# RWKV and HGRN steps placed between the W_in GEMMs by a clock instead of a table: a hybrid decoder layer on one core

## The chip, the cores and the metric

One core of one Trainium2 chip runs the whole step. The metric is the device time of one execution in microseconds (us). The kernel before was run three times; the profile shown is of one further execution with the profiler on.

## The reference

One decoder layer for 512 prompt tokens and 8 sequences of 4 sample tokens, all in f32 (D_MODEL 1024):

```
h = RMSNorm(x)
u = h @ W_in                      # 46 blocks of 128 columns: q,f,i,g | r,k,v, low-rank | gates
o_a = HGRN2(u_a)                  # 4 heads, state 128x128, chunkwise gated recurrence
o_b = RWKV7(u_b, h_prev)          # 8 heads, state 64x64, delta-rule update, group norm, gate
x = x + (sig(g_a)*(o_a @ W_a_out) + sig(g_b)*(o_b @ W_b_out)) @ W_out
x = x + relu(RMSNorm(x) @ W_up)^2 @ W_down
y = RMSNorm(x)
```

The outputs are y and the new states of both branches.

## The kernel before

**GEMMs.** Tokens lie along the free axis: 544 columns (512 prompt, 32 sample), split in two halves of 272. Each weight block of 128 columns is loaded by SP into a tile of the tag "stage" (NST buffers); `split` (L166) rounds it to `whi` on ACT and writes the rest `wlo = st - whi` on DVE, one pass over 128x1024 each. `gemm_h` (L398) makes three products per block (`h_hi,whi`, `h_hi,wlo`, `h_lo,whi`), so one W_in block (`in_unit`, L410) is 2 halves x 3 products x 8 = 48 matmuls of 128x272 in the type fp32r. There are 46 such units. After them come `half_unit` for W_b_out and W_a_out, then W_out, W_up and W_down (tiles `full_unit_ps` and `pd`).

**Background.** Between these GEMMs the two recurrences run as small f32 matmuls (32 to 128 wide) with much DVE, ACT and some POOL work. They are Python generators that yield after each step. RWKV goes in two groups of two head pairs (`rw_all`, L990): `rw_batch` (inputs and head sums), `rw_inverse` (triangular inverses on DVE), `rw_solve`, `rw_affine`, `rw_chain` (L793, eight chunk steps that each depend on the last, then the outputs `rw_chain_py`), `gn` (group norm on DVE) and `rw_out`, which stores the branch output to the DRAM tile `ob_d`. HGRN goes by head (`hg_head`, L1080): a scan, seven levels of `decayed` on DVE, score matmuls `hg_head_pl`, and an output stored to `oa_d`. `rw_sample` and `hg_sample` do the sample tokens.

**Order of the work.** `ORDER` (L50) is a table written by hand: unit tokens (`k0`, `f2`, `G8`), tokens that append a generator to lane X or Y (`+rw0`, `+hg1`), and rates (`=25`: two steps of X and five of Y after each unit). `pump` (L1282) resumes the lanes by these rates. That fixes the order in which the program is written; the scheduler of the language then orders the instructions of every engine, PE included, by its own priorities and readiness, so that on PE matmuls of a unit and of the background alternate. The b phase (`half_unit` on `ob_d`, via `branch`, which reloads from DRAM and splits again) starts when all of X is pumped, and takes NPB steps of Y per unit; the a phase on `oa_d` follows.

## Time and profile before

| | us |
|---|---|
| runs | 1003.13, 1004.82, 1006.86 (median 1004.82) |
| the profiled execution, own time | 1008.61 |
| its span in the profile | 1006.9 |
| PE busy | 956.8 |
| DVE busy | 574.0 |
| ACT busy | 411.5 |
| POOL busy | 122.4 |

The span is what the instructions' records cover; the own time is what the same execution took on the device and lies 1.7 us above it. PE is the matmul engine, DVE the vector, ACT the scalar and POOL the GpSimd engine, SP issues DMAs. A f32 matmul leaves two records in the trace, an fp32r matmul one. "PEclk" is the clock granted to PE as a share of its full 2.4 GHz.

### The profile page before, as it was taken

What the parts mean: (1) busy time and instruction counts of PE and PEld (TensorE: products, weight loads), DVE (VectorE), ACT (ScalarE), POOL (GpSimd) and SP (SyncE); (2) the same over time, 40 slices, a digit from 0 to 9 for tenths busy, and PEclk for the clock granted to TensorE, in tenths of its full rate; (3) what the DMA queues carried; (4) which work ended last, traced back from release to release, by engine and by line L of the source; (5) the groups of instructions that cost most, each with busy time, mean ns of one, the idle gap of its engine ahead of it and who ended that gap; (6) DMA issues with size and microseconds to landing.
All of it is one profiled execution on the core that took longest, in us unless ns stands there. A gap on an engine that the chain in (4) does not pass through costs nothing.

```text
span 1006.9 us, 21967 instructions
## 1 busy us (share of the span) xinstructions
PE 956.8 (95%) x9220; PEld 912.1 (91%) x9220; DVE 574.0 (57%) x1150; ACT 411.5 (41%) x765; POOL 122.4 (12%) x300
## 2 busy tenths in 40 slices
PE   5999998899998999999899999999999999999996
PEld 4989888798998888887789999999999999999995
DVE  6634988666786863786877655444222244445433
ACT  7555546543368541352343333334111133333232
POOL 3487231101131200010000000000000000000000
PEclk9999999899999999999998999999999999999998
DMA  8633232322334421445814642233322333334211
GB/s 260 163 136 111 66 93 42 77 61 61 113 121 118 91 68 45 139 144 167 261 63 149 192 129 84 85 86 91 97 84 85 85 87 96 90 105 133 57 43 47
DMA packets 191092, 106.40 MB, mean 106 GB/s; under 512 B 38945, under 2 KB 179047, under 8 KB 190994
## 3 DMA queue, kind: packets, MB, share of 16 engines
q1 hardware_dynamic: 165424, 95.16, 32.5%
q10 hardware_dynamic: 25570, 9.85, 3.8%
q8 instruction: 72, 1.18, 0.5%
q14 instruction: 26, 0.21, 0.1%
HBM read 85.08 MB, written 18.39 MB: 103 GB/s over the span
## 4 chain that ended last, share of the span: by engine, by line
PE 70%; DVE 8%; DMA 3%; ACT 2%; issue 1%; POOL 1%; SPq 0%; ACTq 0%; DVEq 0%; POOLq 0%
PE pd L129 24%; PE full_unit_ps L129 19%; PE in_unit_ps L129 13%; PE half_unit_ps L129 4%; DVE tmp L135 2%; PE rw_chain_py L129 2%; DVE wlo L135 1%; PE rw_chain_ps L129 1%; DMA s0A<-in_state_hgrn_dram 1%; PE rw_affine_pw L129 1%; DVE bn L730 1%; PE rw_affine_pq L129 1%; PE hg_head_po L129 1%; DMA ox<-oa_d 1%; ACT L132 1%
## 5 line engine op out<-in xcount | busy, mean ns | idle before, releaser
L132 ACT ACTIVATE whi<-st 128x1024 fp32r<-128x1024 f32 x120 | 126.9, 1057 | 254.1 <-PE pd L129 119.6
L135 DVE TENSOR_TENSOR wlo<-st,whi 128x1024 fp32r<-128x1024 f32 x120 | 148.0, 1234 | 133.9 <-PE full_unit_ps L129 40.3
L129 PE MATMUL in_unit_ps<-h_hi,whi 128*128 128x272 f32 (+3 forms) x736 | 120.6, 299 | 4.9 <-ACT xk L132 2.1
L129 PE MATMUL in_unit_ps<-h_lo,whi 128*128 128x272 f32 (+3 forms) x736 | 117.7, 295 | 0.0
L129 PE MATMUL in_unit_ps<-h_hi,wlo 128*128 128x272 f32 (+3 forms) x736 | 116.3, 294 | 0.2 <-DVE wlo L135 0.2
L129 PEld LDWEIGHTS in_unit_ps<-h_hi,whi 128*128 128x128 f32 x736 | 101.9, 191 | 10.2 <-issue 3.1
L129 PE MATMUL full_unit_ps<-hd,whi 128*128 128x272 f32 (+2 forms) x832 | 110.4, 289 | 0.0
L129 PEld LDWEIGHTS full_unit_ps<-hd,whi 128*128 128x128 f32 x832 | 106.6, 189 | 0.0
L129 PEld LDWEIGHTS in_unit_ps<-h_lo,whi 128*128 128x128 f32 x736 | 102.0, 191 | 3.0 <-issue 1.7
L129 PEld LDWEIGHTS in_unit_ps<-h_hi,wlo 128*128 128x128 f32 x736 | 100.7, 190 | 3.3 <-issue 1.9
L129 PE MATMUL pd<-xgl,whi 128*128 128x272 f32 x512 | 70.3, 289 | 0.0
L129 PE MATMUL pd<-xgh,wlo 128*128 128x272 f32 x512 | 70.0, 288 | 0.0
L129 PE MATMUL pd<-xgh,whi 128*128 128x272 f32 x512 | 70.0, 289 | 0.0
L129 PEld LDWEIGHTS pd<-xgl,whi 128*128 128x128 f32 x512 | 66.8, 188 | 0.0
L129 PEld LDWEIGHTS pd<-xgh,whi 128*128 128x128 f32 x512 | 66.3, 188 | 0.0
L129 PEld LDWEIGHTS pd<-xgh,wlo 128*128 128x128 f32 x512 | 66.2, 188 | 0.0
L141 POOL TENSOR_SCALAR ys<-ys,ssf 32x512 f32<-32x512 f32 x1 | 1.1, 1085 | 492.5 <-DVE ssf L1507 492.5
L129 PE MATMUL full_unit_ps<-hd,wlo 128*128 128x272 f32 (+2 forms) x416 | 56.6, 288 | 0.0
L129 PEld LDWEIGHTS full_unit_ps<-hd,wlo 128*128 128x128 f32 x416 | 53.9, 188 | 0.0
L135 DVE TENSOR_TENSOR hd<-r,hd 128x544 fp32r<-128x544 f32 x32 | 23.2, 726 | 47.9 <-ACT hd L132 47.9
L135 DVE TENSOR_TENSOR x<-x,full_unit_ps 128x272 f32<-128x272 f32 (+2 forms) x48 | 19.6, 435 | 37.4 <-PE full_unit_ps L129 37.4
L138 DVE SCALAR_TENSOR_TENSOR r<-pd,rsb 128x272 f32<-128x272 f32 x64 | 25.2, 436 | 25.5 <-PE pd L129 23.5
(416 smaller groups left out, 1506.1 us busy)
## 6 DMA issues: line engine op xcount, KB each, us to landing
st<-in_w_in_dram SPq DMA_DIRECT2D x46, 512.0 KB
st<-in_w_up_dram SPq DMA_DIRECT2D x32, 512.0 KB
st<-in_w_down_dram SPq DMA_DIRECT2D x32, 512.0 KB
gt_d<-gt SPq DMA_DIRECT2D x16, 272.0 KB
st<-in_w_out_dram SPq DMA_DIRECT2D x8, 512.0 KB
gtb<-gt_d SPq DMA_DIRECT2D x8, 272.0 KB
gta<-gt_d SPq DMA_DIRECT2D x8, 272.0 KB
x<-xt_d SPq DMA_DIRECT2D x8, 272.0 KB
```

Of the source, the lines that this page charges most:

```text
L129: T.matmul(out, lhsT, rhs, start=start, stop=stop)
L132: A.activation(out=out, in_=in_, func=func, **kw)
L135: (eng or V).tensor_tensor(out=out, in0=a, in1=b, op=op)
L138: V.scalar_tensor_tensor(out=out, in0=a, scalar=s, in1=b, op0=op0, op1=op1)
L141: (eng or V).tensor_scalar(out=out, in0=a, scalar1=s1, scalar2=s2, op0=op0, op1=op1)
L730: V.tensor_reduce(out=o_[:, i0:i1, t0:t1], in_=tp, axis=AX.X, op=ALU.add)
```

## The change

**A clock of its own.** V, A, P, T and the DMA queues are wrapped in `Timed`. Each call issues the real instruction and books its cost, by small formulas, on `Clock`: a time line per engine, and for each tile when it is ready and last used. PE's line only moves forward. From the first W_in unit to the end of the b phase PE's instructions stay in the order in which they are written (`manual_schedule` for PE); the other engines are scheduled as before.

**Who runs when.** `gemm_h` calls `tick` after every 4 matmuls for the steps marked SOFT and after every 12 for all. `tick` resumes each of three lanes (LX for RWKV, LZ for the low-rank part and the token-wise RWKV work, LY for HGRN and samples) whose next step is ready by the clock. A generator yields WAIT while a unit that it needs is not there. `choose` takes the next unit from NEED while the pool of 12 unit outputs has room, else from FILL.

**Longer steps.** `rw_chain` makes the input products of all eight chunks in one run (`rw_chain_pc`), then per chunk only the two state products; `rw_chain_py` makes all inputs, then all state products. `rw_solve` takes both pairs at once, `rw_affine` overlaps neighbours, `hg_head` computes five levels before one run of `hg_head_pl`, `rw_sample` and `hg_sample` prepare operands a step ahead.

**Weights.** The first 11 W_in units keep `wlo` on DVE; for the other 35 it goes to POOL. Loads go three units ahead and splits two ahead (`ahead`); "stage" has 3 buffers instead of 4, "wlo" 3 instead of 2.

**The end.** All four HGRN heads are in the W_in section now; the end of RWKV group 1 and `hg_sample` come last. After the last unit `drain(LX, LZ)` empties these lanes; LY's rest runs in the b phase and is drained behind it. The count of matmuls is the same.

```diff
-NST = 4
+NST = 3
...
-PULL = 5
-NPB = 9
-NPX, NPY = 8, 9
-ORDER = """l0 l1 k1 c1 v1 +lo k0 c0 r0 v0 c2 r3 r1 +rw0 v3 q0 =25 f0 i0 i3 g0 +hg0 f1 i1 g1 k3 q1 +hg1 v2 G8 k2 G10
-r2 +rw1 +rs =34 i2 g3 q2 G2 G1 f2 f3 =52 q3 G3 =93 G7 g2 +hs +hg3x G13 G4 G11 G15 G9 G12 G5 G6 G14 =56 +hg2 G0"""
+QUANT, FINE = 12, 4
+NDVE = 11
+NEED = "l0 k0 k1 r0 v0 r1 v1 l1 f0 q0 i0 g0 f1 q1 i1 g1 f2 q2 i2 g2 k2 k3 r2 r3 v2 v3 f3 q3 i3 g3"
+FILL = "G8 G10 G2 G1 G3 G7 G13 G4 G11 G15 G9 G12 G5 G6 G14 G0"
+X_WORK = "rw0 rw1"
+Y_WORK = "hg0 hg1 hg2 hg3 rs hs"
...
+    def note(self, eng, cost, outs, ins, lane):
+        for t in outs:
+            self.first(t)
+        r = 0.0
+        for t, own in [(t, False) for t in ins] + [(t, True) for t in outs]:
+            if self.by.get(t.name) != eng or (eng == "DMA" and not own):
+                r = max(r, self.ready.get(t.name, 0.0))
+            elif eng not in ("PE", "DMA"):
+                r = max(r, self.ready[t.name] - 0.12)
+            if own and not (eng in ("PE", "DMA") and self.by.get(t.name) == eng):
+                r = max(r, self.used.get(t.name, 0.0))
+        if eng == "PE":
+            if r > self.pe + 0.2:
+                self.late.append((self.pe, r - self.pe, outs[0].name))
+            self.pe = end = max(self.pe, r) + cost
+            end += 0.15
+        elif eng == "DMA":
+            end = r + cost
+        else:
+            end = self.place(eng, r, cost) + 0.12
...
+            gemm = len(ops) > 1 and ops[1].dtype == F32R
+            switch = 0.12 if gemm != self.clock.gemm else 0.0
+            self.clock.gemm = gemm
+            if gemm:
+                return n / 2400 + 0.013 + switch
...
+        if fn == "dma_start":
+            return 2.3
...
+            return 0.15 + 0.00106 * big
+        if self.name == "A":
+            return 0.17 + 0.0009 * big
+        if fn == "tensor_tensor":
+            return 0.2 + 0.0025 * big
+        return 0.3 + 0.0012 * big
...
-    def split(st):
+    def split(st, eng=None):
         w = W()
         w.hi = pipe.tile([128, 1024], F32R, tag="whi", name=nm("whi"))
-        w.lo = pipe.tile([128, 1024], F32R, tag="wlo", name=nm("wlo"), bufs=2)
+        w.lo = pipe.tile([128, 1024], F32R, tag="wlo", name=nm("wlo"), bufs=3)
         act(w.hi, st)
-        tt(w.lo, st, w.hi.bitcast(F32), ALU.subtract)
+        tt(w.lo, st, w.hi.bitcast(F32), ALU.subtract, eng)
...
+                    if (s * K + k + 1) % FINE == 0:
+                        tick((s * K + k + 1) % QUANT == 0)
...
+    def choose():
+
+        if need and (held[0] + (1, 2)[need[0][0] == "f"] + 3 <= NS_O or not fill):
+            if need[0][0] != "l":
+                held[0] += (1, 2)[need[0][0] == "f"]
+            return need.pop(0)
+        return fill.pop(0) if fill else None
...
+    def ahead(c):
+
+        for n, tok in enumerate(plan[0:3]):
+            if tok not in loaded:
+                loaded[tok] = load8(i["w_in"][0], column(tok))
+        for tok in plan[0:2]:
+            if tok in loaded and column(tok) not in weights:
+                weights[column(tok)] = split(loaded[tok], P if len(loaded) > NDVE else V)
+        return weights.pop(c)
...
-        for n in range(8):
+
+        def inputs(out, p, e, n, c, first, last):
+            for h, r in enumerate(hs):
+                mm(out[r], CB[p, n // 4, h][:, n % 4, c], VU[g, n // 2][:, n % 2, e, h, :], first, last)
+
+
+        pc_ = pe("rw_chain_pc").rearrange("p j (n e w) -> p j n e w", n=4, e=2)
+        for j in range(2):
+            for n in range(4):
+                for e, p in enumerate(pairs):
+                    inputs(pc_[:, j, n, e], p, e, 4 * j + n, slice(0, 64), n + e == 0, n == 3 and e == 1)
+            for e, p in enumerate(pairs):
+                tt(ST[j][:, :, e], pc_[:, j, :, e], bc(pcs[:, p, 4 * j:4 * j + 4], 2, 64), ALU.mult)
+        yield
+        for n in range(1, 8):
             ps = LX.one("rw_chain_ps")[:, 0:128].rearrange("p (e w) -> p e w", e=2)
-            vu = VU[g, n // 2][:, n % 2]
             for e, p in enumerate(pairs):
-                for h, r in enumerate(hs):
-                    mm(ps[r, e, :], CB[p, n // 4, h][:, n % 4, 0:64], vu[:, e, h, :], e == 0, e == 1 and n == 0)
-            if n:
-                for e, p in enumerate(pairs):
-                    for r in hs:
-                        mm(ps[r, e, :], GQ[p, n // 4][r, n % 4, 0:64], ST[(n - 1) // 4][r, (n - 1) % 4, e, :], False, e == 1)
-            tt(ST[n // 4][:, n % 4], ps, bc(pcs[:, 2 * g:2 * g + 2, n], 2, 64), ALU.mult)
+                for r in hs:
+                    mm(ps[r, e, :], GQ[p, n // 4][r, n % 4, 0:64], ST[(n - 1) // 4][r, (n - 1) % 4, e, :], e == 0, e == 1)
+            for e, p in enumerate(pairs):
+                st = ST[n // 4][:, n % 4, e, :]
+                stt(st, ps[:, e, :], pcs[:, p, n:n + 1], st, ALU.mult, ALU.add)
             yield
+        py_ = [t.rearrange("p (n w) -> p n w", w=64) for t in LX.two("rw_chain_py")]
         for e, p in enumerate(pairs):
-            py_ = LX.one("rw_chain_py").rearrange("p (n w) -> p n w", w=64)
             for n in range(8):
-                for h, r in enumerate(hs):
-                    mm(py_[r, n, :], CB[p, n // 4, h][:, n % 4, 64:128], VU[g, n // 2][:, n % 2, e, h, :], True, n == 0)
-                if n:
-                    for r in hs:
-                        mm(py_[r, n, :], GQ[p, n // 4][r, n % 4, 64:128], ST[(n - 1) // 4][r, (n - 1) % 4, e, :], False, True)
+                inputs(py_[e][:, n], p, e, n, slice(64, 128), n == 0, False)
+        for e, p in enumerate(pairs):
+            for n in range(1, 8):
+                for r in hs:
+                    mm(py_[e][r, n, :], GQ[p, n // 4][r, n % 4, 64:128], ST[(n - 1) // 4][r, (n - 1) % 4, e, :], False, n == 7)
             yo[p] = S(512, name="yo").rearrange("p (n w) -> p n w", w=64)
-            act(yo[p], py_)
-            yield
+            act(yo[p], py_[e])
...
+        for hw in (16, 8, 4, 2, 1):
+            level(hw)
+            yield None if hw == 1 else SOFT
...
+    def tick(all_=True):
+
+
+        again = True
+        while again:
+            again = False
+            for L in lanes:
+                if L.work and L.ready <= clock.pe and (all_ or L.soft):
+                    again = advance(L) or again
...
+    region = tc.manual_schedule(engines={mybir.EngineType.PE})
+    region.__enter__()
+    clock.start()
...
+        done.add(tok)
+    drain(LX, LZ)
...
-            pump(0, NPB)
-    while pump1(LY):
-        pass
+    drain(LY)
+    region.__exit__(None, None, None)
...
```

On PE, in the middle of the W_in section before: two chunk steps of the first `rw_chain` (`rw_chain_ps`, numbered by chunk) beside the matmuls of a unit.

```order
L129 MATMUL rw_chain_ps712_5154<-VU613_4309,CB548_3934 64x64
L129 MATMUL rw_chain_ps712_5154<-VU613_4309,CB549_3937 64x64
L129 MATMUL rw_chain_ps712_5154<-VU613_4309,CB588_4167 64x64
L129 MATMUL rw_chain_ps712_5154<-VU613_4309,CB589_4170 64x64
L129 MATMUL in_unit_ps757_5513<-h_hi_132,whi754_5484 128x272 x2
L129 MATMUL rw_chain_ps712_5154<-st699_5040,GQ684_4953 64x64 x2
L129 MATMUL rw_chain_ps712_5154<-st699_5040,GQ698_5037 64x64 x2
L129 MATMUL rw_chain_ps713_5164<-VU613_4309,CB548_3934 64x64
L129 MATMUL rw_chain_ps713_5164<-VU613_4309,CB549_3937 64x64
L129 MATMUL rw_chain_ps713_5164<-VU613_4309,CB588_4167 64x64
L129 MATMUL rw_chain_ps713_5164<-VU613_4309,CB589_4170 64x64
L129 MATMUL in_unit_ps757_5513<-h_hi_132,whi754_5484 128x272 x2
```

The same place of the changed kernel, where `in_unit_ps445` and `452` are the two halves of units.

```order
L160 MATMUL in_unit_ps445_3242<-h_hi_132,wlo401_2900 128x272 x4
L160 MATMUL rw_chain_ps446_3255<-st418_3024,GQ392_2846 64x64 x2
L160 MATMUL rw_chain_ps446_3255<-st418_3024,GQ415_2995 64x64 x2
L160 MATMUL in_unit_ps445_3242<-h_hi_132,wlo401_2900 128x272 x4
L160 MATMUL in_unit_ps445_3242<-h_lo_133,whi400_2899 128x272 x8
L160 MATMUL rw_chain_ps447_3274<-st418_3024,GQ392_2846 64x64 x2
L160 MATMUL rw_chain_ps447_3274<-st418_3024,GQ415_2995 64x64 x2
L160 MATMUL in_unit_ps452_3291<-h_hi_132,whi423_3076 128x272 x8
L160 MATMUL in_unit_ps452_3291<-h_hi_132,wlo424_3077 128x272 x4
L160 MATMUL rw_chain_ps453_3304<-st418_3024,GQ392_2846 64x64 x2
L160 MATMUL rw_chain_ps453_3304<-st418_3024,GQ415_2995 64x64 x2
```

The four input products (`VU,CB`) are gone from each step, and the GEMM is left at every chunk for four state products, after 12 matmuls there instead of after 2.

On PE at the end of the W_in section before, where `in_unit_ps891` is the last half of the last unit and `half_unit_ps919` the first of the b phase.

```order
L129 MATMUL in_unit_ps891_6460<-h_hi_132,whi888_6431 128x272 x8
L129 MATMUL in_unit_ps891_6460<-h_hi_132,wlo889_6432 128x272 x8
L129 MATMUL in_unit_ps891_6460<-h_lo_133,whi888_6431 128x272 x8
L1266 MATMUL hg_sample_pt874_6302<-ident_93,hs797_5803 128x128
L129 MATMUL hg_head_pl894_6491<-X898_6496 32x32 x8
L129 MATMUL half_unit_ps919_6588<-oh904_6558,whi916_6582 128x272
L129 MATMUL half_unit_ps920_6601<-oh904_6558,whi916_6582 128x272
```

The same place of the changed kernel (of the rows between, one stands for each kind of step).

```order
L160 MATMUL in_unit_ps842_6273<-h_lo_133,whi802_5913 128x272 x8
L160 MATMUL rw_chain_ps848_6323<-st820_6060,GQ806_5939 64x64 x2
...
L160 MATMUL rw_sample_pn849_6330<-um846_6302,rs774_5641 64x512 x2
...
L160 MATMUL rw_chain_py853_6348<-VU671_4835,CB615_4463 64x64
...
L160 MATMUL rw_chain_py853_6348<-st820_6060,GQ817_6034 64x64 x6
...
L160 MATMUL rw_sample_pt857_6416<-ident_93,s0T762_5553 128x128 x4
...
L160 MATMUL hg_sample_pl876_6511<-ga_429 32x32 x4
...
L160 MATMUL rw_out_pt882_6543<-ident_93,yo854_6395 64x64 x16
...
L160 MATMUL hg_sample_pt888_6593<-ident_93,x3878_6529 96x128 x4
...
L160 MATMUL hg_sample_po892_6607<-s0A895_6616,sqm893_6608 32x128
...
L160 MATMUL hg_sample_po892_6607<-s0A898_6619,sqm894_6609 32x128
L160 MATMUL half_unit_ps919_6691<-oh901_6655,whi913_6679 128x272
```

Before, the b phase follows the last unit after one transpose and the first score matmuls of the last head. Now the last chunk step, the outputs of the chain, `rw_out` and the head of `hg_sample` stand between the two.

On DVE in that same stretch of the changed kernel: from the last state of the chain to the last product for `ob_d` (of 55 rows, those that mark the way).

```order
L160 TENSOR_TENSOR um852_6346<-rs776_5643,bmk_342 128x512
L160 TENSOR_REDUCE gs1859_6429<-yo854_6395 128x8
...
L160 TENSOR_TENSOR yo854_6395<-yo854_6395,gs1859_6429 128x512
L160 TENSOR_TENSOR wlo932_6768<-st930_6765,whi931_6767 128x1024
...
L160 TENSOR_REDUCE gs2861_6435<-gsq860_6433 128x8
...
L160 TENSOR_TENSOR yo855_6411<-yo855_6411,gs1871_6488 128x512
...
L160 SCALAR_TENSOR_TENSOR rs863_6438<-rs863_6438,gs2861_6435 128x8
...
L160 TENSOR_TENSOR yo854_6395<-yo854_6395,gs2861_6435 128x512
...
L160 TENSOR_REDUCE gs2873_6494<-gsq872_6492 128x8
...
L160 TENSOR_TENSOR yo855_6411<-yo855_6411,gs2873_6494 128x512
L160 TENSOR_TENSOR og884_6563<-og884_6563,bv604_4390 128x512
...
L160 TENSOR_TENSOR og887_6588<-og887_6588,gB886_6585 128x512
```

Before, these rows of the second chain lay among the last units' rows; now they stand behind the last unit, with one `wlo` and `hg_sample`'s rows between them.

On POOL of the changed kernel, in the middle of the W_in section.

```order
L160 TENSOR_TENSOR wlo315_2139<-st275_1773,whi314_2138 128x1024
L160 COPY el311_2122<-qh309_2117 128x4
L160 TENSOR_TENSOR wlo325_2226<-st313_2136,whi324_2225 128x1024
...
L160 TENSOR_TENSOR wlo336_2324<-st323_2223,whi335_2323 128x1024
L160 MEMSET att368_2640 128x512
...
L160 TENSOR_TENSOR wlo344_2396<-st334_2321,whi343_2395 128x1024
...
L160 TENSOR_TENSOR wlo355_2475<-st342_2393,whi354_2474 128x1024
...
L160 TENSOR_TENSOR wlo363_2609<-st353_2472,whi362_2608 128x1024
```

Before, POOL had no `wlo`, only copies, sets to zero and some narrower products; DVE had all of them.

## Rows read from the trace of the kernel before

**Rows 1.** Page, part 1: busy us of each engine, share of the span, instructions.

```profile
PE 956.8 (95%) x9220; PEld 912.1 (91%) x9220; DVE 574.0 (57%) x1150; ACT 411.5 (41%) x765; POOL 122.4 (12%) x300
```

**Rows 2.** Windows: W_in, b phase, a phase, the rest; columns as the first line says.

```profile
core 0: us, PE busy (x) PEld busy (x) DVE busy (x) ACT busy (x) POOL busy (x), PEclk, DMA share, GB/s
17.50:486.70 469.20, 445.46 (x5041) 406.64 (x5039) 322.44 (x695) 231.21 (x447) 116.19 (x283) 0.99 0.38 106
486.70:530.50 43.80, 36.72 (x450) 33.52 (x449) 32.99 (x80) 18.37 (x36) 1.54 (x5) 0.95 0.49 160
530.50:556.70 26.20, 26.13 (x188) 26.13 (x189) 21.05 (x46) 9.63 (x14) 0.00 (x0) 0.89 0.44 138
556.70:1006.90 450.20, 440.64 (x3512) 439.62 (x3510) 187.78 (x298) 141.35 (x242) 1.08 (x1) 0.99 0.32 93
```

**Rows 3.** Windows of five stretches with a low granted clock (PEclk, third column from the right).

```profile
113.20:116.60 3.40, 3.12 (x14) 3.12 (x15) 3.40 (x3) 2.99 (x4) 0.50 (x2) 0.51 0.55 159
178.00:184.80 6.80, 4.42 (x33) 4.07 (x34) 6.74 (x13) 3.92 (x7) 3.48 (x8) 0.50 0.71 169
468.10:471.50 3.40, 3.40 (x14) 2.10 (x12) 2.31 (x7) 0.62 (x2) 0.00 (x0) 0.51 0.89 279
492.00:495.40 3.40, 3.11 (x42) 2.73 (x43) 2.48 (x6) 1.19 (x2) 0.00 (x0) 0.50 1.04 350
529.60:536.40 6.80, 5.83 (x25) 5.83 (x26) 2.47 (x5) 1.31 (x2) 0.00 (x0) 0.50 0.97 338
```

**Rows 4.** Waits of PE, 17.5 to 556.7: us in total, times, longest us.

```profile
PE hg_head_pu L129 <- DVE X L135: 5.6, 4, 4.5
...
PE in_unit_ps L129 <- ACT h_hi L132: 1.4, 1, 1.4
PE in_unit_ps L129 <- ACT U L132: 1.3, 1, 1.3
...
PE in_unit_ps L129 <- DVE wlo L135: 0.2, 1, 0.2
```

**Rows 5.** Timeline of PE around 205 us: start us, us, instruction, count.

```profile
204.59 0.65 PE L129 MATMUL in_unit_ps<-h_lo,whi 128*128 128x272 f32 x3
205.08 0.66 PE L129 MATMUL in_unit_ps<-h_hi,whi 128*128 128x276 f32 x4
205.67 0.55 PE L129 MATMUL rw_affine_pq<-CB,W 64*64 64x128 f32 x6
```

**Rows 6.** Chain of waits: start us, us, engine, tile, records.

```profile
396.34 7.61 PE rw_chain_py L129 x120
...
615.62 87.64 PE pd L129 x695
```

**Rows 7.** Timeline of PE inside the first `rw_chain_py`.

```profile
400.07 0.45 PE L129 MATMUL rw_chain_py<-VU,CB 128*64 128x64 f32 x8
400.45 0.33 PE L129 MATMUL rw_chain_py<-st,GQ 64*64 64x64 f32 x4
```

**Rows 8.** Timeline of DVE around 410 us: group norm of the first chain.

```profile
410.30 0.17 DVE L138 SCALAR_TENSOR_TENSOR rs<-rs,rs 128x8 f32<-128x8 f32 x1
410.50 0.17 DVE L135 TENSOR_TENSOR rs<-rs 128x8 f32<-128x8 f32 x1
410.74 0.69 DVE L135 TENSOR_TENSOR s0T<-rw_sample_pn,s0T 128x512 f32<-128x512 f32 x1
411.35 0.16 DVE L138 SCALAR_TENSOR_TENSOR rs<-rs,gs 128x8 f32<-128x8 f32 x1
```

**Rows 9.** Timeline: last HGRN output on DVE, first matmul of the a phase.

```profile
524.04 0.75 DVE L138 SCALAR_TENSOR_TENSOR hog<-hg_head_pt,prm,xq 128x512 f32<-128x512 f32 x1 [0.75 <-PE hg_head_pt L1171]
...
530.57 0.82 PE L129 MATMUL half_unit_ps<-oh,whi 128*128 128x272 f32 x2 [2.60 <-ACT oh L132]
```

**Rows 10.** Timeline of DVE and POOL: two `wlo`, and POOL's `sxl`.

```profile
118.18 1.22 DVE L135 TENSOR_TENSOR wlo<-st,whi 128x1024 fp32r<-128x1024 f32 x1 [0.35 <-PE in_unit_ps L129]
...
134.67 1.34 POOL L135 TENSOR_TENSOR sxl<-rk,sxh 128x544 fp32r<-128x544 f32 x1 [0.67 <-POOL gs L600]
...
135.21 1.88 DVE L135 TENSOR_TENSOR wlo<-st,whi 128x1024 fp32r<-128x1024 f32 x1
```

More of the change, by code (lines that the diff above doesn't have):

```diff
@@ L514, in hybrid_step, with low_rank @@
     sig, al = {}, {}
-    def first_pairs():
-        for p in range(4):
-            gB = S(TOK, name="gB")
-            act(h2(gB), lora(2, p))
-            DQ.dma_start(out=gb_d[:, p, :], in_=gB)
-            yield
+    def low_rank():
+        while "l0" not in done:
+            yield WAIT
+        yield clock.at(*wa_l, *wa_h)
         for p in (0, 1):
@@ L549, in rw_batch @@
         nrm, sqp = {}, {}
+        while not all(p in xk for p in pairs):
+            yield WAIT
+        yield clock.at(*(xk[p] for p in pairs))
         for p in pairs:
@@ L988, in hybrid_step, with rw_sample_out @@
+    def rw_sample_out():
+        while "rs" not in done or len(fin) < 4:
+            yield WAIT
+        tt(gs[:, 6], gs[:, 6], gs[:, 7], ALU.mult)
+        DQ.dma_start(out=ob_d[:, :, SEQ:TOK], in_=gs[:, 6])
     xk, xr, xv = {}, {}, {}
@@ L996, in meanwhile @@
                 yield from rw_tokens(p)
[L998 to L1005 removed]
+        LZ.ready = max(LZ.ready, LX.end)
+        LZ.work.append(meanwhile())
+        yield from rw_inverse(g)
+        yield SOFT
+        yield from rw_solve(pairs)
+        while LZ.work:
+            yield WAIT
         yield from rw_affine(g)
@@ L1174, in hg_head @@
         DQ.dma_start(out=oa_d[:, h, 0:SEQ], in_=og)
+        held[0] -= 1
         yield
     def hg_sample(L):
+        while not all(f"g{h}" in done for h in range(4)):
+            yield WAIT
+        yield
         q, lf, k, v, g = (ga[:, a].rearrange("p h t -> p (h t)") for a in range(5))
```

571 lines of the change are left out of this document (351 added, 220 removed).

## The prediction

> **What bounds the kernel now.** The page's totals come first [rows 1]: PE is busy 956.8 of 1006.9 us (95%), and the next engine, DVE, 57%. So this is one long PE queue: a change pays only if it shortens PE's own work, fills its idle time, or keeps its clock up; what it does to another engine counts where PE waits for it. The table by stage [rows 2] then says where anything can be had. From 556.7 us on, 450.2 us run code that the change leaves as it is: no term. In the W_in section PE is idle for 469.20 - 445.46 = 23.7 us, in the b phase for 43.80 - 36.72 = 7.1, in the a phase for 0.1. The granted clock stands at half (0.50 to 0.51, that is 1.2 instead of 2.4 GHz) in five stretches, 23.8 us together [rows 3]; half of each is lost, 6.8 us in the W_in section and 5.1 at the end of the b phase. Idle and half clock together are 42.7 us, 4.2% of the span. The waits of PE [rows 4] are many small ones: the largest group is 5.6 us (one of 4.5) for DVE's levels of an HGRN head; 1.4 + 1.3 us are waits for the first activations, and a weight's low part is waited for once, 0.2 us. Last, the timeline tells what it costs to alternate. A GEMM matmul in a long run takes 87.64/695 = 0.126 us [rows 6]. Three of them after background work take 204.59 to 205.08 = 0.49 us, so 0.11 more than 3 x 0.126, and the four before the next background work 0.59, so 0.09 more than 4 x 0.126 [rows 5]. A visit of the background thus costs about 0.2 us beside its own matmuls.
>
> **Visits.** The order of PE before has 117 runs of background matmuls between GEMM runs up to the end of the b phase, the changed one 69. 48 x 0.2 = **9.6 us** less, all on PE. Bounds: 0, if the extra time at the joints is a wait for operands that only moves; 15 if a joint costs as much as 0.3.
>
> **The chain in runs.** `rw_chain_py` has 120 records in 7.61 us [rows 6], groups of four that alternate between two kinds of operands, 0.25 us a group. Where eight of one kind follow one another they take 400.07 to 400.45 = 0.38 us [rows 7], so 0.13 for four more, 0.03 a record. In runs, 120 records are about 0.25 + 116 x 0.03 = 3.8; with the joints that stay I take 3.9, and 2 x (7.61 - 3.9) = **7.4 us** less over the two groups. The inputs of `rw_chain_ps`, 16 groups of four, go into a run too: 16 x 0.13 = 2.1, I take **2**. Bounds for both together: 0 (the run of eight is one case) to 11.
>
> **Waits and clock in the W_in section.** Idle 23.7 and half clock 6.8 make 30.5 us that a better order could take. The start-up waits (2.7) stay. The clock's prices are near the rows for DVE (a `wlo` is 0.15 + 1024 x 0.00106 = 1.24, the row 1.22 [rows 10]), so that a step is resumed when its operands are about there; but DMAs have one price whatever their size, and DVE and POOL are scheduled by other rules than PE. I take it that half goes: 15 stay, **15.5 less**. Bounds: 0 (as many new waits as old ones go) to 27.8.
>
> **The end of the W_in section.** This speaks against the change. Before, the b phase follows the last unit at once, and what is lost there is the 7.1 us idle and 5.1 half clock of the b phase: 12.2. Now the end of RWKV group 1 lies behind the last unit. From the last unit to the first matmul of the b phase go: the last chunk step, `rw_chain_py` and its copy, about 4.4 us; then on DVE the 55 rows of the excerpt up to the last product for `ob_d`, namely 13 wide ones at 0.61, one `wlo` at 1.2, 26 small ones at 0.2 start to start and 15 in between at about 0.25, some 18 us [rows 8, 10]; then store, reload, split and matmul, which before took from 524.04 + 0.75 = 524.79 to 530.57 = 5.8 us [rows 9]. Together 28 us, in which PE has about 12 of its own work: 16 idle. At the end of the b phase `hg_sample` closes in the same manner: its norm, a `wlo`, the products and the same 5.8 us, about 12 us, nearly all idle (11). With 3 of waits inside the b phase and 6 for the low clock that follows such pauses [rows 3, 9], the end costs 36 instead of 12.2: **23.8 more**. Bounds: 8 more, if the small rows overlap with ACT's steps as the clock plans and PE's background fills the gap; 32, if the levels of the norm wait for one another.
>
> **Low parts on POOL.** For 35 units the 1.22 us of DVE go (43 us of its 322 in this section [rows 2]). On POOL, 544 columns take 1.34 us [rows 10], so 1024 would take about 2.5: 35 x 2.5 = 88 us on an engine busy 116 of 469 us [rows 2]. A unit of 48 matmuls lasts 48 x 0.126 = 6 us, and the split is written a unit ahead; so it is hidden behind one unit, and I cost it at zero. Without that cover it is 2.5 - 1.2 = 1.3 us x 35 = 45 us, the upper bound; below, the relief of DVE is already in the waits above.
>
> **Fewer stage buffers, one more for low parts.** A load has two units, 12 us, to land, and PE waited just 0.2 us for a low part before [rows 4]: zero, bounds 0 to 5.
>
> **Sum.** -9.6 - 7.4 - 2 - 15.5 + 23.8 = -10.7 us. Made against the profiled execution's own time, 1008.61, it gives 997.9; that execution lies 3.8 us above the median of the runs, 1004.82, and the same sum there gives **994**. A measurement of this kernel tells some 0.5%, 5 us, from no change.
>
> **Rivals.** *POOL holds DVE up (slower).* The row: POOL's `sxl` ran from 134.67 to 136.01, a `wlo` on DVE started at 135.21 beside it and took 1.88 us, 0.66 more than the 1.22 of the other [rows 10]; it seems to have stood still for most of the overlap. The changed POOL does 35 such passes of about 2.5 us, 88 us, against 43 taken from DVE, and most of DVE's work in this section (levels, masks, group norms) reads two tiles from SBUF. A DVE step on the path to PE's next matmul that is caught loses up to 2.5 us. It decides from the point where 4 or 5 of the 35 whole holds reach PE (10.7/2.5 = 4.3 takes up the gain). If one in four did, 9 x 2.5 = 22 us: 994 + 22 = 1016. For it: DVE is busy 69% of this section. Against: PE waited for POOL's or DVE's late work in few places, and steps are resumed only when the clock thinks them done. Chance 0.24.
> [...]
> *The ends eat the gain (same).* The pauses behind the last unit and behind the b phase come out at the upper bound (8 more than I took) or only a few of the old waits go (12 of them stay more): -10.7 + 10 = about 0, 1004. For it: group norm is a chain of small rows of which each waits for the last [rows 8]. Against: `rw_sample` and `hg_sample` give PE work in that time. Chance 0.20.
> *The waits nearly vanish (faster still).* If 3 of the 30.5 us stay and the end costs 20 instead of 36 with the two chains interleaved, that is up to 28 more, and 15 of it brings 979. For it: that the order of PE is now written with the same prices that the other engines have. Against: DVE and POOL do not follow this order. Chance 0.14.
> That the change does not do what it says is excluded for the visits by the order itself (69 against 117); for the rest it is the rival of the ends.
>
> **Numbers.** The forecast (986 to 1000) has 0.42. Faster than 999.8: 0.42 + 0.14 = 0.56; between 999.8 and 1009.8: 0.20; slower: 0.24. The range leaves out the upper half of the POOL case and the lower half of the last one, 0.12 + 0.07: 979 to 1014.
>
> **What would show it.** Right: a busy PE in the W_in section that is some 17 us shorter; a `rw_chain_py` run of about 4 us; PE's idle time there at 15 or less; a pause of PE of 15 us or more, with a half clock behind it, ahead of the first `half_unit`, and one of about 11 ahead of the a phase; `wlo` on POOL at about 2.5 us. Wrong: DVE's two-tile rows much longer than before while a POOL `wlo` runs, and PE waits put down to them or to `wlo` (POOL); waits of PE spread over the section that are longer than before; or pauses at the ends of a few us only.

## The result and the profile after

The changed kernel takes 1108.7 us (median of 4 runs, 1101.6 to 1110.2), the kernel before 1005.8 (4 runs): a ratio of 1.099, 95% interval 1.092 to 1.107. It is 10% slower; the forecast was 994, with 1014 as the upper end. The profiled execution is the one of 1101.6 us.

The engines' totals and the table by stage of the changed kernel, with the same columns as [rows 1] and [rows 2]. The stages are: first to last W_in unit, from there to the first `half_unit`, b phase, a phase, rest.

```profile
PE 957.2 (87%) x9220; PEld 923.6 (84%) x9220; DVE 577.3 (52%) x1135; ACT 404.9 (37%) x761; POOL 198.5 (18%) x335
```

```profile
17.50:540.65 523.15, 429.57 (x4959) 407.48 (x4960) 309.68 (x627) 222.85 (x440) 191.12 (x314) 0.92 0.29 82
540.65:574.68 34.03, 18.40 (x280) 12.97 (x279) 20.11 (x65) 11.24 (x25) 2.75 (x9) 0.71 0.54 146
574.68:622.50 47.82, 33.83 (x242) 31.14 (x242) 29.80 (x64) 7.30 (x12) 0.00 (x0) 0.79 0.50 161
622.50:649.20 26.70, 26.31 (x194) 25.99 (x195) 22.12 (x47) 10.10 (x15) 0.00 (x0) 0.92 0.42 139
649.20:1099.90 450.70, 440.15 (x3511) 438.49 (x3509) 186.53 (x298) 141.54 (x243) 1.09 (x1) 0.99 0.32 93
```

The rest is as before (450.7 against 450.2 us [rows 2]), so all of the loss lies ahead of it: it starts at 649.2 instead of 556.7, 92.5 us later. In the W_in section PE is idle for 523.15 - 429.57 = 93.6 us, before 23.7. Behind it PE is idle for 15.6 + 14.0 + 0.4 = 30.0, before 7.1. So 92.7 us more idle time. Listed as in [rows 3], the stretches at half clock up to 649 us add up to 133 us instead of 23.8; half of PE's busy time in those, the estimate used here for what the clock takes, is 39 us, before 10. And 29.6 less is PE's own work: busy time up to that point less the loss to the clock is 508.1 - 39.4 = 468.7 us against 508.3 - 10.0 = 498.3. The sum is 92.7 + 29.4 - 29.6 = 92.5. PE got less to do, as forecast; it waits for it.

The waits of PE in the changed kernel (columns as in [rows 4]):

```profile
PE hg_head_pt L160 <- DVE kh L160: 16.3, 4, 7.7
PE hg_head_pt L160 <- DVE hy L160: 16.1, 3, 8.2
PE lora_ps L160 <- DVE CB L160: 14.6, 2, 12.9
PE half_unit_ps L160 <- ACT oh L160: 11.3, 5, 6.4
PE head_sums_ps L160 <- POOL sxl L160: 6.9, 2, 6.2
PE rw_state_ps L160 <- DMA sn<-in_state_wkv_dram: 6.4, 1, 6.4
PE hg_sample_pl L160 <- DVE hs L160: 6.1, 1, 6.1
```

Before, the longest was 4.5 us. No line names `wlo`: the low parts from POOL came in time. Three of these pauses can be followed to their source.

**The first: 12.95 us, at 115 us.** Timelines of PE, DVE and POOL of the changed kernel.

```profile
115.24 0.79 PE L160 MATMUL lora_ps<-lx,lwh 128*128 128x272 f32 x2 [12.95 <-DVE CB L160]
```

```profile
95.48 0.69 DVE L160 TENSOR_TENSOR d<-U 128x511 f32<-128x511 f32 x1 [1.10 <-ACT U L160]
109.89 0.79 DVE L160 SCALAR_TENSOR_TENSOR xm<-d,prm,U 128x544 f32<-128x544 f32 x1 [13.72 <-POOL d L160]
```

```profile
95.69 0.82 POOL L394 TENSOR_SCALAR_AFFINE_SELECT lmk<-lmk 32x32 f32<-32x32 f32 x2
...
107.69 1.69 POOL L394 TENSOR_SCALAR_AFFINE_SELECT lmk<-lmk 32x32 f32<-32x32 f32 x6
109.46 0.40 POOL L160 TENSOR_TENSOR d<-U 128x24 f32<-128x24 f32 x2
```

PE waits for DVE, DVE stood still for 13.72 us for POOL's part of `d` (the sample tokens, 0.40 us), and POOL was writing masks from 90 to 109 us: `consts2`, a block of some 65 small rows that the change emits before the eighth unit. It goes to POOL through a wrapper of its own that calls the engine directly (L394), so the clock books none of it. The pause of 6.2 us for `sxl` at 145 us follows `consts3` (135 to 144 us on POOL) in the same way.

**The second: a POOL low part beside DVE.** Timelines of DVE and POOL of the changed kernel.

```profile
321.38 0.79 DVE L160 SCALAR_TENSOR_TENSOR xm<-d,prm,U 128x544 f32<-128x544 f32 x1
...
328.21 2.84 DVE L160 SCALAR_TENSOR_TENSOR xm<-d,prm,U 128x544 f32<-128x544 f32 x1 [2.87 <-POOL d L160]
330.97 0.68 DVE L160 TENSOR_TENSOR kh<-hb 128x512 f32<-128x512 f32 x1
```

```profile
324.76 3.06 POOL L160 TENSOR_TENSOR sxl<-sq,sxh 128x544 fp32r<-128x544 f32 x2
...
328.13 2.34 POOL L160 TENSOR_TENSOR wlo<-st,whi 128x1024 fp32r<-128x1024 f32 x1
```

The same `xm` takes 0.79 us alone and 2.84 us when it starts 0.08 us behind a `wlo` of 2.34 us on POOL; it ends 0.58 us behind that. `kh` comes behind it, and PE's longest wait for `kh` (7.7 us) ends soon after. The hold is 2.05 us of that wait; before it DVE stood still for 2.87 us until POOL's part of `d` was done, which had two `sxl` ahead of it. In the 3.88 us wait for `hy` at 212 us the hold is the larger part: one step of the norm takes 2.24 us instead of 0.16.

```profile
208.23 2.24 DVE L160 SCALAR_TENSOR_TENSOR rs<-rs,ss_h 128x4 f32<-128x4 f32 x1
```

```profile
208.11 2.34 POOL L160 TENSOR_TENSOR wlo<-st,whi 128x1024 fp32r<-128x1024 f32 x1 [4.39 <-ACT whi L160]
```

Over the whole trace, 47 DVE rows start while a `wlo` runs on POOL; 21 of them take longer than such rows do alone, by 34.8 us in sum.

**The third: small rows between wide ones.** Timeline of DVE ahead of the 8.2 us wait for `hy`.

```profile
353.36 0.15 DVE L160 TENSOR_SCALAR rs<-ss_h 128x4 int32<-128x4 int32 x1
353.43 0.77 DVE L160 SCALAR_TENSOR_TENSOR kkn<-xm,prm,nrm 128x544 f32<-128x544 f32 x1
354.13 0.15 DVE L160 TENSOR_SCALAR rs<-rs 128x4 int32<-128x4 int32 x1
354.20 0.77 DVE L160 SCALAR_TENSOR_TENSOR xm<-d,prm,U 128x544 f32<-128x544 f32 x1
354.89 0.18 DVE L160 TENSOR_TENSOR rs<-rs 128x4 f32<-128x4 f32 x1
...
359.98 0.15 DVE L160 SCALAR_TENSOR_TENSOR ss_h<-rs,rs 128x4 f32<-128x4 f32 x1
360.05 0.41 DVE L160 TENSOR_TENSOR eb<-al,b 128x256 f32<-128x256 f32 x1
360.39 0.68 DVE L160 TENSOR_TENSOR hy<-hy,ss_h 128x512 f32<-128x512 f32 x1
```

The norm of an HGRN head is a row of steps on four columns, each 0.15 us long; here they come every 0.8 us, because a wide row of another lane stands between any two; in the norm at 207 us, where DVE had nothing else to do, they came every 0.2 us. The clock books such a step at 0.15 and lets it slip into any gap of DVE. This pause has a second source: the first step of the same norm had been held for 2 us by a `wlo` (the lines are in the last section). With no `wlo` on POOL it was still 5.8 us long.

### The profile page after: what moved, and what is told of

Read it like the earlier page. It is cut to its first block, busy times and chain, and to the rows that moved or that the text cites. A ratio compares the mean times of both kernels' runs of the same rounds, so it can differ in the third digit from the quotient of the medians.

```text
span 1099.9 us, 21956 instructions
## 1 busy us (share of the span) xinstructions
PE 957.2 (87%) x9220; PEld 923.6 (84%) x9220; DVE 577.3 (52%) x1135; ACT 404.9 (37%) x761; POOL 198.5 (18%) x335
## 3 DMA queue, kind: packets, MB, share of 16 engines
q1 hardware_dynamic: 165424, 95.16, 29.6%
## 4 chain that ended last, share of the span: by engine, by line
PE 62%; DVE 15%; DMA 7%; ACT 7%; POOL 4%; issue 4%; SPq 1%; ACTq 1%; POOLq 0%; DVEq 0%
PE pd L160 21%; PE full_unit_ps L160 14%; PE in_unit_ps L160 14%; PE half_unit_ps L160 3%; DVE tmp L160 2%; DMA st<-in_w_down_dram 2%; ACT whi L160 1%; POOL lmk L394 1%; DVE wlo L160 1%; ACT L160 1%; DVE X L160 1%; DVE rs L160 1%; DVE bn L160 1%; PE lora_ps L160 1%; SPq L160 1%
## 5 line engine op out<-in xcount | busy, mean ns | idle before, releaser
L160 DVE TENSOR_TENSOR wlo<-st,whi 128x1024 fp32r<-128x1024 f32 x85 | 104.1, 1225 | 65.9 <-ACT whi L160 65.8
L160 PE MATMUL in_unit_ps<-h_hi,wlo 128*128 128x272 f32 (+3 forms) x736 | 122.2, 302 | 0.0
L160 PE MATMUL in_unit_ps<-h_hi,whi 128*128 128x272 f32 (+3 forms) x736 | 117.7, 304 | 3.5 <-ACT h_hi L160 3.3
L160 PE MATMUL in_unit_ps<-h_lo,whi 128*128 128x272 f32 (+3 forms) x736 | 111.6, 295 | 0.0
L160 PEld LDWEIGHTS in_unit_ps<-h_hi,whi 128*128 128x128 f32 x736 | 104.8, 200 | 5.4 <-ACT h_hi L160 3.8
L160 PEld LDWEIGHTS in_unit_ps<-h_hi,wlo 128*128 128x128 f32 x736 | 105.3, 197 | 2.0 <-issue 0.3
L160 POOL TENSOR_TENSOR wlo<-st,whi 128x1024 fp32r<-128x1024 f32 x35 | 85.8, 2451 | 98.6 <-ACT whi L160 97.4
```

Of the source, the lines that this page charges most:

```text
L160: r = real(*a, **kw)
```

## The experiments

A time without an interval is that of one execution; the kernel before took 1006 to 1010 us beside them. The changed kernel was not run again: gains over it are counted from 1101.6 us, its profiled execution and the fastest of its four, and are 7 us larger from their median. As these four lie 9 us apart, a single difference smaller than that shows nothing. In the expectations, 'port' is the name of one theory, that DVE's rows are held up while a low part runs on POOL: the first rival of the prediction.

**Masks earlier.**

```diff
-        if count in (3, 7, 10):
-            (consts1, consts2, consts3)[(3, 7, 10).index(count)]()
+        if count in (1, 3, 5):
+            (consts2, consts1, consts3)[(1, 3, 5).index(count)]()
```

> The changed kernel (1108.7 us) with the masks written on POOL earlier: consts2 after unit 1, consts1 after 3, consts3 after 5, instead of consts1, 2, 3 after 3, 7, 10. Theory 'POOL queue': the 65 mask rows (91 to 109 us in the changed kernel), which the clock does not book, stood ahead of d and sxl on POOL; the pauses of PE of 12.9 us at 115 and of 6.2 at 145 go, with half of the 20.5 and 6.8 us at half clock: about 19 + 13 = 32 us less, 1076. Rival 'port' and rival 'fixed order': these pauses go elsewhere or are short without it, 0 to 8 us less.

1101.96 us: no gain. The pauses at 115 and 145 us are gone, but PE now waits 14.96 us at 57 us, where `lora_ps` needs `lx`. That is made from DVE's `xm`, and DVE stood still for 13.11 us until POOL, behind the same block of masks, had done its part of `d`. The block only met other steps. The theory missed; the time is as the rivals said, though only because the pause moved.

**Low parts back on DVE.** NDVE = 99.

> The changed kernel with every low part on DVE again (NDVE 99 instead of 11), all else as changed. Theory 'port': DVE's rows with two tiles from SBUF, stretched by some 45 us in sum beside POOL's low parts, come back to their single times (xm 0.78 instead of 1.38, X 0.43 instead of 0.73), and the waits of PE for kh, hy and xm shrink: 30 to 60 us less, 1050 to 1080. Rival 'fixed order': DVE is as busy as before the edit (43 us of low parts come back for the 45 that go), the waits stay: within 10 us of 1108. If the relief of DVE was worth something: slower than 1115.

1076.3 us, 25 less, but the plan moved as well: the W_in section ends at 469 us instead of 541, and 93 us instead of 34 lie between the last unit and the b phase, so this run alone doesn't price POOL.

**PE's order free.** Without `manual_schedule`.

> The changed kernel without manual_schedule: PE's order is again the scheduler's, the program is written as changed. Theory 'fixed order': PE passes what is late with matmuls that are ready; idle time in the W_in section falls from 94 us to 30 or less and the half clock with it: 1010 to 1030. Rival 'port' and 'POOL queue': what PE waits for is late in any order; since the next GEMM matmuls are always ready, part of it is passed, but DVE stays behind: 1050 to 1090.

1081.8 us, 20 less. Idle time in the W_in section is 76 us instead of 94. With a free order PE is still late for most of it: the fixed order is not the main cause while POOL stands in the way.

**Both of the first two.**

> Both edits of the first two runs together. If 'POOL queue' and 'port' each hold and do not meet in the same pauses, their gains add (about 32 + 30 to 60, 1020 to 1050). If one of them pays alone, this run shows that one's gain and no more. 'Fixed order': 1070 to 1108.

1073.8 us: the gain of the second alone (2.5 us apart). The masks' block stalls wherever it is: PE waits 14.26 us at 55 us.

**Low parts on DVE with the same plan.** The real instruction goes to DVE, the clock books it on POOL, so that PE's order stays.

```diff
+    VP = Timed(nc.vector, "P", clock)
-                weights[column(tok)] = split(loaded[tok], P if len(loaded) > NDVE else V)
+                weights[column(tok)] = split(loaded[tok], VP if len(loaded) > NDVE else V)
```

> The changed kernel with all low parts on DVE, but booked on the clock as if on POOL, so that PE's written order stays as it is (with NDVE 99 the plan itself moved: 93 us between the last unit and the b phase instead of 34). Theory 'port': DVE's stretched rows come back to single times and wait less for POOL's in-order queue; idle time of PE in the W_in section falls from 94 to about 60 us and the pauses at the end stay about 30: 1050 to 1060. Rival 'DVE order' (the waits come from small steps that DVE takes in turn with wide ones of another lane, whatever POOL does): the low parts come back to DVE, the waits for kh and hy stay at some 30 us: 1090 to 1110.

1081.2 us, 20 less than the profiled execution of the changed kernel. DVE's rows are back at their single times (`xm` 0.81, `X` 0.42 us). The waits for `kh` fell from 16.3 to 6.2, for `hy` from 16.1 to 10.3. The time lies between the two ranges, and both theories hold in part: the low parts on POOL cost 20 us although DVE got 43 us of work back, and the rest of the waits stays without them. They could cost this by holding up DVE's rows or by filling POOL's queue. In the W_in section DVE's waits for POOL are 21.5 us in the changed kernel and 20.2 here, PE's are 6.9 and 6.8, so the queue has little part in it: what fell is the time of DVE's own rows.

**The same and PE free.**

> As the run before, and PE's order left to the scheduler. Theory 'fixed order and port together': the idle time in the W_in section comes near the 24 us of before: 1010 to 1025. If the program as it is written now (runs of work, ends late) is the cause: 1040 to 1060, near the run before.

1041.9 us, 39 less than the run before, and in the second range: the idle time in the W_in section is 45 us. With POOL out of the way the fixed order is worth twice what it was (20). Two of the remaining pauses are `sxl` behind masks (13.4 and 4.9 us).

**The kernel before with low parts on POOL.**

```diff
+            nsplit[0] += 1
+            w = split(load8(i["w_in"][0], c), P if nsplit[0] > 10 else None)
```

> The kernel before with the low parts of the last 35 units on POOL, nothing else. Theory 'port': DVE's rows beside them are stretched as in the changed kernel, 40 to 50 us in sum, and POOL's other steps wait behind low parts; PE waits more, its order being fixed at compile time too: 1025 to 1050. Rival 'the clock's order alone is late': POOL has time for it, 1000 to 1012.

1042.5 us, 33 slower than before. Without clock, lanes or fixed order, this part of the change alone costs 3%. One line of the groups by line, of the kernel before, and then of this run:

```profile
L135 DVE TENSOR_TENSOR X<-xk,E 128x256 f32<-128x256 f32 x28 | 12.0, 427 | 7.4 <-ACT E L132 7.4
```

```profile
L135 DVE TENSOR_TENSOR X<-xk,E 128x256 f32<-128x256 f32 x28 | 20.7, 739 | 11.8 <-ACT E L132 11.8
L135 POOL TENSOR_TENSOR wlo<-st,whi 128x1024 fp32r<-128x1024 f32 x35 | 85.8, 2451 | 156.3 <-PE in_unit_ps L129 99.2 <-ACT gsq L132 24.1 <-issue 17.9
```

The second number behind the bar is the mean of one in ns: `X` went from 427 to 739 beside low parts of 2451. One wait of PE in this run, with the rows of DVE and POOL that it goes back to:

```profile
109.46 2.91 DVE L135 TENSOR_TENSOR eb<-al,b 128x256 f32<-128x256 f32 x2
114.75 0.69 PE L129 MATMUL head_sums_ps<-sxh,bones 128*128 128x272 f32 x2 [4.70 <-ACT sxh L132]
```

```profile
109.58 2.52 POOL L135 TENSOR_TENSOR wlo<-st,whi 128x1024 fp32r<-128x1024 f32 x1
```

Two `eb` take 0.77 us in the kernel before; here the second ends at 112.37, 0.27 us behind POOL's `wlo`, 2.1 us later than with two of the usual length. From there DVE is busy without a pause up to `rk`, ACT rounds that to `sxh`, and PE starts. So a hold does reach PE.

**Masks in small steps.** `consts1` to `3` became one generator that yields after each block of a level, resumed after every 12 matmuls; low parts on DVE with the same plan, and PE's order fixed.

```diff
+                        if (s * K + k + 1) % QUANT == 0:
+                            next(mask_steps, None)
```

> As the first run of this call, with the masks written on POOL in 33 small steps, one after every 12 matmuls from the second unit on, instead of three blocks. Theory 'POOL queue': neither lx nor d nor sxl stands behind a block of masks; the pauses of 13 to 15 us and 6 us shrink to 2 or 3 us each, with the half clock about 20 to 28 us less than the first run of this call. Rival: POOL is full in that stretch in any case, the pause moves once more (as it moved from 115 to 57 us when the blocks came earlier): within 6 us of it.

1060.5 us, 20.7 less than with the blocks (1081.2). The pause at 115 us is down to 2.1, that for `sxl` at 145 is gone, the first one for `lx` (5.8) stays.

**All three, and the ends.**

> Three edits together: low parts on DVE (booked as POOL), masks in 33 small steps, PE's order left to the scheduler; units and lanes in the changed order. If the three causes add as they did one by one (25, 21 and 39 us off 1102): 1015 to 1025, and what is left over the kernel before is the end of the W_in section (some 30 us idle there in all runs so far). If freeing PE already hid the mask pauses: 1035 to 1042.

1024.0 us, as the sum said. Table by stage (W_in, to the first `half_unit`, b, a):

```profile
19.40:470.90 451.50, 420.86 (x4956) 397.01 (x4954) 307.45 (x659) 220.94 (x437) 120.59 (x279) 0.97 0.34 95
470.90:502.30 31.40, 17.52 (x282) 12.94 (x281) 21.17 (x67) 10.98 (x25) 2.46 (x9) 0.73 0.55 159
502.30:543.30 41.00, 29.91 (x240) 28.05 (x240) 28.29 (x61) 7.15 (x11) 0.00 (x0) 0.87 0.60 186
543.30:571.30 28.00, 27.68 (x194) 27.10 (x195) 22.32 (x47) 10.24 (x15) 0.00 (x0) 0.88 0.43 139
```

The W_in section is now shorter than before (ends at 470.9 instead of 486.7) and idle for 30.6 us against 23.7; but 13.9 + 11.1 + 0.3 = 25.3 us are idle behind it. Three other orders of units and lanes were tried on this version:

```diff
-NEED = "l0 k0 k1 r0 v0 r1 v1 l1 f0 q0 i0 g0 f1 q1 i1 g1 f2 q2 i2 g2 k2 k3 r2 r3 v2 v3 f3 q3 i3 g3"
+NEED = "l0 k0 k1 r0 v0 r1 v1 l1 f0 q0 i0 g0 f1 q1 i1 g1 k2 k3 r2 r3 v2 v3 f2 q2 i2 g2 f3 q3 i3 g3"
-Y_WORK = "hg0 hg1 hg2 hg3 rs hs"
+Y_WORK = "hg0 hg1 hg2 rs hs hg3"
```

> As the run before, and the ends put back: NEED takes k2 k3 r2 r3 v2 v3 before the third HGRN head's units, and head 3 comes last, after hg_sample, so that it falls into the b phase as a head did before. In PE's order the first half_unit then follows the last unit at once (one row, instead of 74). Theory 'ends': the pauses behind the last unit and ahead of the a phase (14 and 11 us idle with some 8 of half clock in the run with low parts on DVE and PE free) fall to the 7 of before: 25 us less than the run before, 985 to 1000, below the kernel before. Rival: they only move into the W_in section, whose lanes are then more crowded: within 8 us of the run before.

1041.8 us: the first `half_unit` follows 2.8 us behind the last unit, but head 3 then stands alone in the b and a phases, with 12.0 and 16.4 us idle. It is 18 us slower than the run before, which neither the theory nor its rival had.

With `Y_WORK = "hg0 hg1 rs hg2 hg3 hs"`:

> As the run with three edits and PE free (1024 us), with NEED taking k2 k3 r2 r3 v2 v3 before head 2's units and lane Y in the order hg0 hg1 rs hg2 hg3 hs. In PE's order 15 background matmuls stand between the last unit and the first half_unit (152 in that run), 70 after it (28). Theory 'ends': the pause behind the last unit goes, the one ahead of the a phase stays: 1005 to 1013. Rival (the work at the end is a chain of fixed length that only shows elsewhere, as when head 3 came last): 1020 to 1040.

1023.6: the pause behind the last unit is 1.3 us, the b phase is idle for 17.9 us (of 58.7). With head 3 on lane X and `"hg0 hg1 hg2 rs hs"`:

> As the run with three edits and PE free, the same NEED, head 3 on lane X behind rw1 and Y as hg0 hg1 hg2 rs hs: 168 background matmuls behind the last unit, none in the b phase. Theory 'ends': one pause instead of two, the a phase follows the b phase at once: about 11 us idle and 4 of half clock less, 1005 to 1012. Rival (the one pause becomes as long as the two were): 1020 to 1030.

1031.9: one stretch with 23.7 us idle in 47.6 us, next to nothing after. The theory failed each time, and the second time the rival held (the third lies 2 us above its range). The idle time behind the last unit was 25.3 us in the order of the change and 31.2, 19.8 and 24.1 in these three: the end looks like a chain of nearly fixed length that shows where it is put. Which order would hide it was not found.

The first of these orders with PE fixed, and with nothing else of the edits:

> As the run before with PE's order fixed again (manual_schedule). Theory 'fixed order': 25 to 40 us slower than the run before, with PE waiting for DVE's kh and hy rows. Rival (the clock's order is good once nothing unbooked is in its way): within 10 us of it.

> The changed kernel with the order of units and lanes of the two runs before alone (low parts on POOL, masks in blocks, PE fixed). Prices the end by itself: the forecast's term for it was 23.8 us, so 1078 to 1088; within 8 us of 1102 if the work only stalls elsewhere.

1079.4 and 1104.9 us. The fixed order costs 38 us here, as it did before (39 and 37). On the changed kernel the new order of units gains nothing.

**The longer chain steps on the kernel before.** `rw_chain` as in the change, all else as before.

> The kernel before with the changed rw_chain alone (inputs in runs, then the state products), same number of steps, PE's order left to the scheduler. The forecast's term: rw_chain_py 7.4 us and rw_chain_ps 2 us less on PE: 995 to 998 against 1005. Rival (the time of a record is the same in runs, the extra was waiting for operands): 1003 to 1008. Slower than 1008: the seven state steps, now two rows on DVE each, lengthen the chain's way.

996.4 us (994.9 to 997.6, 4 runs) against 1007.3 (7 runs): ratio 0.988, interval 0.987 to 0.990. This is 1.2% below the kernel before, small but clear of the noise. From start to start, without what was waited, `rw_chain_py` takes 15.2 us before, 7.8 here; in the changed kernel 7.9, where the first group reads:

```profile
289.30 2.09 PE L160 MATMUL rw_chain_py<-VU,CB 128*64 128x64 f32 x64
291.31 1.03 PE L160 MATMUL rw_chain_py<-st,GQ 64*64 64x64 f32 x28
293.72 1.03 PE L160 MATMUL rw_chain_py<-st,GQ 64*64 64x64 f32 x28 [1.37 <-ACT yo L160]
```

64 records in 2.01 us are 0.031 a record, as forecast from the run of eight in [rows 7]. The range held, but in part by luck: `rw_chain_pc` and `rw_chain_ps` together take 11.5 us here, and the inputs and states took 11.4 before, so the 2 us for them did not come. In the profiled executions PE's busy time less the loss to the clock fell by 5.5 us, its idle time by 4.0, and the first unit started 1.2 us earlier.

**Small DVE steps booked longer, masks alone.**

```diff
-            return 0.15 + 0.00106 * big
+            return (0.65 if big <= 8 else 0.15) + 0.00106 * big
```

> As the run with low parts on DVE, masks in small steps and PE fixed (1060.5 us), with one more edit on the clock: a DVE step of at most 8 columns is booked at 0.65 us instead of 0.15, since in the changed kernel's trace such rows stand in turn with wide rows of another lane and come about every 0.8 us. Theory 'DVE order': PE no longer reaches hg_head_pt before hy is there; the waits for hy (three, 9.8 us in that run) fall under 4 us. The plan moves as well (486 background matmuls behind the last unit instead of 151), so the total is not compared with the theory: 1045 to 1085. Rival (the lateness has another source): the waits for hy stay at 8 us or more.

The waits for `hy` went from 9.8 to 0.9 us, as the theory on the third pause said; since the plan moved too, this bears that cause out and does not prove it. The time is 1081.0, since this plan leaves 99 us between the last unit and the b phase.

> The changed kernel (low parts on POOL, PE fixed) with the masks in 33 small steps alone. Theory 'masks and low parts are two causes that add': 18 to 28 us less than 1102 to 1108, 1078 to 1088. Rival (POOL is so full with low parts that the masks' place does not matter): within 8 us of it.

1094.7 us, 7 less than the profiled execution of the changed kernel, just within the rival's 8 us, and 14 less than its median, between the two expectations. The pauses at 115 and 145 us go here too, and idle time in the W_in section falls by 14.2 us, nearly as with the low parts on DVE (15.2). But the loss to the clock up to the end of the a phase is 46.1 us instead of 39.4, and takes half of it back; it did not rise with the low parts on DVE. Why, no run shows.

## Why the prediction was wrong

**The step that failed is the one on waits and clock in the W_in section.** It said that half of 30.5 us goes and 15 stay. Measured are 93.6 us idle and 27 lost to the clock. Its reason was that the clock's prices are near the rows, so that a step is resumed when its operands are about there. The prices are near, row by row, for the long DVE rows; the operands were late all the same. What the step left out is what the clock doesn't book at all, and what stands between two rows in an engine's queue. The runs divide the way from 1101.6 (the profiled execution) to 1024.0 into three parts: low parts on POOL, by their hold on DVE, 20; masks not booked 21; PE's fixed order 37. They were taken off in this order, one execution each, and are not independent: the fixed order alone was worth 20 to 27 with POOL in the way, the masks alone 7 to 14.

**Visits and chain** were right in kind and too small: 19 us forecast (9.6 + 7.4 + 2), 29.6 measured on PE. The chain's part was 7.4 for `rw_chain_py`, measured 15.2 - 7.9 = 7.3, and 2 for its inputs, measured 11.4 before and 4.5 + 5.1 after, 1.8. So about 20 is left to the fewer visits and the other longer steps, twice the term. The traces have more visits than were counted, and more that go: from the first W_in unit to the end of the b phase, 151 stretches of matmuls that are of no unit before, 89 after, so 62 less and not 48. What one costs can be told from the runs with PE free, which have the same matmuls in 15 to 39 more visits than the same program with PE fixed: their busy time less the loss to the clock is 3.7 to 9.8 us longer, 0.2 to 0.3 us a visit. By these figures 62 visits are an estimated 13 to 21 us, which leaves little for the other steps; no run has the visits alone.

**The end of the W_in section** had its idle time right: 30 us forecast (16, 3 and 11), 30.0 measured (15.6, 14.0 and 0.4, the second pause being counted into the b phase here). The second pause went as described: PE waits 4.7 us for the norm of `hg_sample` and 6.4 for the reload, 11.1 together. The first came out by luck: from the last unit to the first `half_unit` went 34.0 us and not 28, but PE was busy for 18.4 of them and not 12, 5.5 of that lost to the low clock; its longest wait there is 6.1 us for operands of `hg_sample`, which DVE made among the rows of the group norm. The low clock behind the section was sized at 6 and cost 13, so that the end came to 31 us more than before and not 23.8, within the bound of 32.

**Low parts on POOL** were costed at zero since they are made a unit ahead. That cover held: PE never waited for one. But the rival named for it was real: 20 us in the changed kernel, 33 in the kernel before. Its price, 22 us for one whole hold in four that reaches PE, comes near by luck; the trace has 21 rows of DVE held up, for 34.8 us, and how many of them reach PE was not counted. One pair of rows had told it [rows 10], and it was given 0.24. Even with its price the forecast would have been 1016, and not 1109. The trace shows holds in both directions: an `xm` of 0.79 us alone that started 0.08 us behind a `wlo` of 2.34 took 2.84, and a `wlo` that started at 186.26 beside a `tmp` of DVE that ran until 187.25 took 3.26 us, where 32 of the 35 took 2.34 to 2.51. In two places `xm` was held though its record starts 0.01 us ahead of the `wlo` (at 339.90 and 372.08, 2.2 us each), which is too close to tell the order.

**Stage buffers** were right at zero: no wait of PE names a weight's load.

**What was not among the rivals** is the block of masks. The diff shows it: `consts2` moves from behind three units to behind seven, and the wrapper `late` was changed to call POOL directly, past the clock. The step on POOL counted the 35 low parts and not the 65 rows of masks that stand in the same queue at a new place. The forecast followed what moved on PE and DVE and not every row that moved on POOL.

**Half clock.** From 17.5 to 649.2 us PE has 19 pauses of over 2 us: 13 overlap a stretch with a granted clock of 0.50, four end 0.07 to 1.56 us ahead of one, and the two of 3.33 us, at 195 and 451 us, do neither. Behind the 3.88 us wait at 212 us, in a stretch from 210.3 to 217.1 with a granted clock of 0.50, eight GEMM matmuls take 213.02 to 214.98 = 1.96 us, and 1.01 some 5 us later:

```profile
212.26 1.11 PE L160 MATMUL hg_head_pt<-ident,hy 128*128 128x128 f32 x4 [3.88 <-DVE hy L160]
213.02 2.16 PE L160 MATMUL in_unit_ps<-h_hi,whi 128*128 128x272 f32 x8
214.98 2.02 PE L160 MATMUL in_unit_ps<-h_hi,wlo 128*128 128x272 f32 x8
...
217.94 1.17 PE L160 MATMUL in_unit_ps<-h_hi,whi 128*128 128x272 f32 x8
218.95 1.16 PE L160 MATMUL in_unit_ps<-h_hi,wlo 128*128 128x272 f32 x8
```

In runs of the same tile, 272 columns start every 0.227 us at 0.50 and every 0.125 at 1.00 (medians of this trace). So "half" is an estimate a little above the 45% that these show, and the 1.2 GHz of the prediction stands here for 272/0.227 = 1.20 columns a ns. In all, 92.7 us more idle time came with another 29.4 us lost to the clock. The loss does not follow the idle time in a fixed share: with the masks alone in small steps there was 14.2 us less idle time in the W_in section and 6.7 more loss (46.1 against 39.4). The forecast took 11.9 us as lost before, half of each stretch; with PE's busy time in them it is 10.0.

**Still open** are the last 18 us between 1024.0 and the kernel before. By the two traces, up to the end of the a phase, that run has 18 us more idle time at the ends (25.3 against 7.1), 7 more in the W_in section and 12 more lost to the clock, against 22 less of PE's own work. So the pauses at the ends have the size of what is missing, but no order that was tried took them away.

## What to carry to other kernels

Here a plan by a clock of one's own was as good as its worst unbooked instruction: before fixing an engine's order by it, list what goes to each engine past the clock, and compare the booked gap between two dependent steps with their distance in a trace, not only their durations. A pass moved from DVE to POOL was not simply taken off DVE here: of 47 DVE rows that started beside a low part on POOL, 21 took 0.8 to 2.2 us longer than alone. Price such a move as a hold on the DVE rows that it meets, but for the kinds that the next section shows unchanged. Take large changes apart: here one function of the change, put alone into the kernel before, gave 1.2%, while the whole cost 10%.
